# Hybrid encoder layer on one core: x transposed by TensorE, and the first eight projection steps in an order by hand

## The chip, the cores and the metric

The kernel runs on one core of one Trainium2 chip. A core has five engines with instruction streams of their own: TensorE (PE in the profile; its weight loads are shown apart as PEld), VectorE (DVE), ScalarE (ACT), GpSimd (POOL) and SyncE (SP). They meet through semaphores, and they share an on-chip memory (SBUF), the accumulators behind TensorE (PSUM) and the DMA queues to and from HBM. The metric is the device time of one execution, in microseconds (us), over several executions of the same program. Lower is better.

## The reference

One layer of an encoder over 1024 tokens of 1024 features, in float32:

```python
h = rmsnorm(x, norm_gain)
q_a, k_a, v_a, g_a, q_b, k_b, v_b, g_b = split(h @ w_in)     # 512,128,128,512,512,512,512,512
q_a = rmsnorm(q_a by head, q_norm_a); k_a likewise           # 8 query heads, 2 key heads, 64 wide
q_a = q_a * cos + rotate_half(q_a) * sin; k_a likewise       # the rotation
o_a = softmax(q_a k_a^T / 8) v_a * silu(g_a)                 # full attention, 1024 keys
o_b = neighbourhood_attention(q_b, k_b, v_b, rpb) * silu(g_b) # a window of 8 x 16 grid places
x = x + concat(o_a, o_b) @ w_out
return rmsnorm(x, final_norm_gain)
```

Every large product is kept close to float32 by splitting both factors into a float16 value (hi) and the float16 rest (lo), and adding three products: hi by hi, lo by hi, hi by lo.

## The kernel before, in words

**Tiles and groups.** The tokens stand in eight tiles of 128, called x0 to x7. The columns of the weights stand in groups of 256. Group 0 (KVA) makes keys and values of head group A, groups 1 and 2 (QA, QA+1) its queries, four heads each; 3 to 12 make head group B and the gates, 13 to 16 are `w_out`. A projection works on two tokens' tiles at once, called a pair `up` of 0 to 3. One tile takes 3 products x 8 slices of 128 features = 24 matmuls of 128x256, a pair 48, and a pair's 48 are cut into 8 chunks of 6. So "k2" below is group 0 on pair 2 (x4 and x5), and "q2" is group 1 on it. The first pairs come in the order k0, q0, k1, q1, k2, k3, q2, q3, then the four pairs of group 2. TensorE does 72 chunks (nine pairs) before the first score of head group A. In the listings `pj0_3` is the PSUM tile of group 0, pair 3 (k3), `pj1_2` that of q2, `pj2_0` that of the first pair of group 2. Two PSUM banks hold these tiles in turn.

**From x to the projection.** A tile of x is loaded by SP, squared and summed by ACT (L303), turned into a scale by DVE and POOL (L310 to L312), scaled by DVE (L315), rounded to hi by ACT (L316), and the rest is taken by DVE or POOL (L320). Both halves are turned by a DMA transpose on SP's queue (L324) into `hT`, with features on the partitions; there are 16 such DMAs. The weights of a group go through squares (`prep_a`, or L372 in quarters, ACT), a sum on TensorE (L388), a power on POOL (L391), hi on ACT (L397 or L414) and lo on DVE (L404 or L419), and some small DVE work (`prep_e`, L436 to L443).

**From the projection to the score.** When a pair of k or q is done, ACT takes it out of PSUM (L598 for v, L550 copy and L551 squares; part a), DVE sums the squares (L554, L555) and POOL raises them to the power -1/2 (L556; part b). The rotation is part c: a product on DVE (L560), two on POOL (L564, from the tables), one on DVE (L567) and a sum on POOL (L568). Then ACT rounds to hi (L583 for q; L608 and L609 for k), DVE takes the rest (L584; L614), and SP issues a DMA transpose (L587; L620 and L622). The tables of cos and sin are first multiplied by the gains: `tables()` on DVE (L279 to L289), `scale_tab` on POOL (L292, four times). A score of head group A multiplies a tile of queries by the keys of all 1024 tokens (L741, L743), in two halves, so the second matmul of the first score needs the keys of k3. DVE takes its maximum (L748), ACT the exponentials (L752) and their rounding (L753), DVE the rest (L758), SP issues the transpose, and TensorE multiplies by v (L775, L776).

**What sets the order.** `Flow` is the order by hand: slots, one to a pair, and in each slot positions ("pre", "mid", "post", "end"). `at(delay, position, work)` puts work into a later slot, `fill(n)` issues n chunks of matmuls, and `step(n)` runs a whole slot. TensorE's order is always the written one. For the other engines it is the written one inside blocks marked `manual_schedule`; outside, a scheduler orders them by its own estimates. The first pairs are outside. Weights of groups 2 and 3 (1 MB each) are loaded through POOL's queue, held back by a copy on POOL that needs x6 and x5 (`gate`, L220).

## Time and profile before

| what | us |
|---|---|
| three runs | 556.81, 555.02, 556.80 (median 556.8) |
| the profiled execution | 554.79 |
| its span, first to last instruction | 553.0 |
| first matmul of a projection | 14.64 |
| k3's values leave PSUM (ACT, L598) | 69.14 |
| SP issues the transpose of k3's keys (L620) | 76.97 |
| first score (L741) | 87.15 |

The span is the time between the first and the last instruction of the profiled execution; its own time is 1.8 us longer. In listings of groups, a row has the line of the source, the engine, the operation, the tile written and the tile read with their sizes and the count; behind the bar the busy time, the mean of one in ns, and the idle time just ahead of them with what ended it. In a timeline a row begins with its start and its length, rows that follow at once are joined (x8), and the brackets hold the idle time ahead and what ended it. In the table by stretches each engine has its busy time and its number of instructions, then come the granted clock of TensorE, the share of the DMA engines, and GB/s.

### The profile page before, as it was taken

Reading aid. Unit: us, or ns where it says so; the run is one execution under the profiler, and the core shown is the slowest. Engines: PE = TensorE matmul, PEld = TensorE weight load, DVE = VectorE, ACT = ScalarE, POOL = GpSimd, SP = SyncE. Lnnn points to the kernel's source line nnn. Section 1 sums busy time; section 2 is a strip of 40 time slices with the busy share of each in tenths; the row PEclk is TensorE's granted clock in tenths of the full one; section 3 lists DMA queues with packets and bytes.
Section 4 is the critical chain, followed back from the end, with each engine's and each line's share of the span. In section 5 each row is a group of like instructions: output and inputs, shape, how many; then the busy total and the mean of one; then the engine's idle time right before and its main releaser. Section 6 shows DMA issues by size and latency. Waiting matters only on the chain.

```text
span 553.0 us, 12864 instructions
## 1 busy us (share of the span) xinstructions
PE 507.8 (92%) x5071; PEld 397.2 (72%) x5071; DVE 445.3 (81%) x887; ACT 381.4 (69%) x671; POOL 178.9 (32%) x201
## 2 busy tenths in 40 slices
PE   2657889998999999999999999999999998799994
PEld 0446768876887555558888888988777786589883
DVE  4599678889987888879879898867898997887732
ACT  4545465967887868787787696648688788784411
POOL 1385787581110000101000022634433123344510
PEclk9989999999999999999999999999999999999998
DMA  8997837879999999999997999744897799979722
GB/s 243 210 203 216 146 59 181 135 144 176 208 196 217 191 231 186 216 176 178 194 217 143 202 186 200 120 125 71 146 191 138 136 250 202 219 115 204 173 74 76
DMA packets 244509, 95.40 MB, mean 173 GB/s; under 512 B 235489, under 2 KB 236001, under 8 KB 242530
## 3 DMA queue, kind: packets, MB, share of 16 engines
q1 hardware_dynamic: 242434, 81.23, 80.1%
q0 software_dynamic: 1728, 12.58, 7.3%
q8 instruction: 39, 0.64, 0.5%
q10 hardware_dynamic: 288, 0.79, 0.5%
q14 instruction: 20, 0.16, 0.1%
HBM read 29.56 MB, written 4.19 MB: 61 GB/s over the span
## 4 chain that ended last, share of the span: by engine, by line
PE 50%; DVE 10%; ACT 9%; issue 5%; DMA 3%; POOL 0%; DVEq 0%; POOLq 0%; ACTq 0%
PE pj L504 17%; PE kb L504 7%; PE pjb L504 7%; PE pv L775 5%; PE s L741 4%; PE s L743 4%; ACT rq L856 3%; DVE ar L854 3%; ACT ar L858 2%; PE pv L776 2%; PE sb L504 2%; DMA pt<-ar 2%; DVE ar L863 1%; DMA ar<-ar 1%; DVE whl L419 1%
## 5 line engine op out<-in xcount | busy, mean ns | idle before, releaser
L504 PEld LDWEIGHTS <-hT 128*128 128x128 f16 x2112 | 204.2, 99 | 59.5 <-DMA hT<-ar 16.3
L504 PE MATMUL pj<-whl,hT 128*128 128x256 f16 x1680 | 201.7, 278 | 21.8 <-DMA hT<-ar 9.4
L752 ACT ACTIVATE ar<-s,nm,sm 128x1024 f32<-128x1024 f32 x64 | 76.9, 1201 | 47.7 <-DVE nm L748 45.7
L748 DVE CUSTOM_DVE_ANT_0 ar<-s,sm 128x1024 bf16<-128x1024 f32 x64 | 82.0, 1281 | 30.3 <-PE s L743 28.5
L504 PEld LDWEIGHTS <-ar 128*128 128x128 f16 x768 | 73.8, 98 | 16.0 <-issue 7.8
L758 DVE TENSOR_TENSOR ar<-ar 128x1024 f16<-128x1024 f32 x64 | 79.4, 1241 | 1.2 <-ACT ar L753 1.2
L753 ACT ACTIVATE ar<-ar 128x1024 f16<-128x1024 f32 x64 | 67.6, 1057 | 2.3 <-DVE ar L758 0.4
L504 PE MATMUL pjb<-whl,ar 128*128 128x256 f16 x480 | 56.4, 273 | 2.8 <-ACT whl L414 1.5
L856 ACT ACTIVATE rq<-ar,nm 128x384 f32<-128x384 f32 (+1 forms) x64 | 34.0, 579 | 25.7 <-DVE nm L854 25.1
L504 PE MATMUL pjb<-whl,hT 128*128 128x256 f16 x432 | 50.4, 273 | 0.1
L784 POOL TENSOR_TENSOR ar<-ar,sum 128x256 f32<-128x256 f32 x16 | 11.3, 709 | 110.7 <-DVE ar L783 95.3
L504 PE MATMUL kb<-hT,whl 128*128 128x512 f16 x192 | 44.5, 379 | 0.0
L419 DVE SCALAR_TENSOR_TENSOR whl<-raw,sm,whl 128x512 f16<-128x512 f32 x52 | 41.0, 821 | 2.7 <-ACT whl L414 2.7
L775 PE MATMUL pv<-va,ar 128*128 128x128 f16 x384 | 39.1, 220 | 0.0
L863 DVE SCALAR_TENSOR_TENSOR ar<-rq,ar 128x768 f16<-128x768 f32 (+1 forms) x32 | 29.3, 915 | 11.0 <-ACT ar L858 10.6
L741 PE MATMUL s<-kTa,rq 128*128 128x512 f16 x128 | 38.1, 379 | 0.0
L776 PE MATMUL pv<-va,ar 128*128 128x64 f16 x384 | 37.8, 193 | 0.0
L775 PEld LDWEIGHTS <-ar 128*128 128x128 f16 x384 | 33.9, 98 | 5.3
L776 PEld LDWEIGHTS <-ar 128*128 128x128 f16 x384 | 33.2, 98 | 5.3
L414 ACT ACTIVATE whl<-raw,sm 128x512 f16<-128x512 f32 x52 | 34.0, 709 | 1.4 <-POOL sm L391 1.4
L391 POOL TENSOR_TENSOR sm<-wss,mh 128x1 f32<-128x1 f32 x17 | 10.5, 619 | 72.7 <-DVE wss L390 72.7
L910 POOL TENSOR_TENSOR ar<-ar,qkg 128x256 f32<-128x256 f32 x16 | 17.1, 1072 | 51.6 <-DVE qkg L908 36.4
(174 smaller groups left out, 915.9 us busy)
## 6 DMA issues: line engine op xcount, KB each, us to landing
raw<-in_w_dram POOLq DMA_DIRECT2D x11, 1024.0 KB, 7.6
ar<-in_x_dram SPq DMA_DIRECT2D x7, 512.0 KB, 6.1
raw<-in_wo_dram SPq DMA_DIRECT2D x3, 1024.0 KB, 7.0
khh<-ar SPq DMA_DIRECT2D x16, 128.0 KB, 2.7
x2b<-in_x_dram SPq DMA_DIRECT2D x4, 512.0 KB, 7.4
x<-in_x_dram SPq DMA_DIRECT2D x4, 512.0 KB, 5.6
out_dram<-x2b SPq DMA_DIRECT2D x8, 256.0 KB, 4.1
out_dram<-x SPq DMA_DIRECT2D x7, 256.0 KB, 2.9
```

The lines of the kernel that those rows point to most:

```text
L414: act.activation(wp[g][0][:, q], raw[g][:, q], AF.Copy, scale=col(S_ + g))
L419: dve.scalar_tensor_tensor(wp[g][1][:, q], raw[g][:, q], col(S_ + g), wp[g][0][:, q], op0=OP.mult, op1=OP.subtract)
L504: pe.matmul(*o[0], **o[1])
L741: pe.matmul(s[:, c * 512:(c + 1) * 512], q, kTa[:, 4 * c:4 * c + 4, hh], start=True, stop=False)
L748: dve.tensor_tensor_reduce(out=hl[:, 1].bitcast(BF16), in0=s, in1=col(SHA).to_broadcast([P, 1024]), scale=col(NSA), scalar=3e38, op0=OP.ad ...
L752: act.activation(p32, s, AF.Exp, bias=nm, scale=col(SCA), accum_out=rsum[hh, u][:, h:h + 1])
L753: at(0, "mid", lambda: act.activation(hl[:, 0], p32, AF.Copy))
L758: dve.tensor_tensor(hl[:, 1], p32, hl[:, 0], op=OP.subtract)
L775: pe.matmul(o, pt[:, kt], va[:, kt, hh], start=kt == 0, stop=False)
L776: pe.matmul(o[:, :D], pt[:, 8 + kt], va[:, kt, hh, :D], start=False, stop=kt == 7)
L856: act.activation(p32[:, e], t[:, e], AF.Exp, bias=nm, scale=-1.0)
L863: dve.scalar_tensor_tensor(hl[:, 1], p32, 2.0 ** 14, hl[:, 0], op0=OP.mult, op1=OP.subtract)
```

## The change

It has three parts.

1. **TensorE turns x.** For each tile, after the scaling, eight transposes of 128x128 in float32 (`tp`, a matmul against an identity that POOL builds at the start) go into one PSUM tile `xT`, ACT rounds PSUM to the hi half of `hT` in two instructions of 128x512 (`tp_hi`), and DVE subtracts to get the lo half, 128x1024 (`tp_lo`). The 16 DMA transposes, the rounding in SBUF and the subtraction in SBUF are gone. There is one `xT`, so the transposes of a tile follow the `tp_lo` of the tile ahead of it. Twenty matmuls of 128x256 on the identity, whose result nobody reads (`busy`), are issued ahead of the first transposes.
2. **The first eight steps in an order by hand.** Before the loop all engines' work up to the second projection pair is put into `manual_schedule`, and `stage(1)` to `stage(7)` write out where the work of each tile, of the tables and of groups 2 and 3 stands among the chunks. `tables()` and the four `scale_tab` stand behind `tp_lo(6)`, in stage 4. Groups 2 and 3 are loaded through SP's queue, without the copies on POOL; the squares of group 2 come in quarters, and its rounding (`prep_c`, `prep_d`) stands in stage 6, behind k3. The split of group 3 comes behind the first score, where it came ahead of it. Group 4's load is issued by POOL in stage 7.
3. **Rotations later.** `lag` moves part c, and what follows it, by more slots: for keys of pairs 0 to 3 by 4, 2, 1, 1 where it was 0, for queries of group 1 by 3, 2, 1, 1. Part b moves from "mid" to a new position "b" ahead of "post". Group 2 stays.

```diff
-        (sp if "b" in late else pool).dma_start(raw[g], w[g] if g < 13 else wo[g - 13])
+        (sp if "b" in late or g < 4 else pool).dma_start(raw[g], w[g] if g < 13 else wo[g - 13])
...
+    def tp(u, *ks):
+        if not xT:
+            xT.append(ps_s.tile([P, KC, P], F32, tag="s", name="xT"))
+        for k in ks:
+            pe.transpose(xT[0][:, k], xts[u][:, k * P:(k + 1) * P], ident)
+
+    def tp_hi(u, half):
+        ks = slice(4 * half, 4 * half + 4)
+        act.activation(hT[0][:, ks, u * P:(u + 1) * P], xT[0][:, ks], AF.Copy)
+
+    def tp_lo(u):
+        cs = slice(u * P, (u + 1) * P)
+        dve.tensor_tensor(hT[1][:, :, cs], xT[0], hT[0][:, :, cs], op=OP.subtract)
+
+    def busy(n):
+        b = ident.bitcast(BF16)
+        for _ in range(n):
+            pe.matmul(spare[0][:, :256], b[:, :P], b, start=True, stop=True)
...
+    def lag(g, up):
+        return 1 if g > QA else {KVA: (4, 2, 1, 1), QA: (3, 2, 1, 1)}[g][up]
...
-        at(1, "post" if g == QA + 1 else "mid", b)
-        at(2 if g == QA + 1 else 1, "post", c)
+        at(1, "post" if g == QA + 1 else "b", b)
+        at(1 + lag(g, up), "post", c)
...
-                at(2, "pre", hi)
+                at(2 + lag(KVA, up), "pre", hi)
...
+            if i == 4:
+                yield "pre mid b"
+                x_scale(7)
+                yield 2
+                tp(6, *range(8))
+                split_t(6)
+                tables()
+                for k in (2, 3, 0, 1):
+                    scale_tab(k)
+                yield "post"
+                yield 6
+            if i == 5:
+                tp(7, *range(8))
+                yield "pre mid"
+                split_t(7)
+                yield "post b"
+                yield 8
+            if i == 6:
+                yield "pre"
+                prep_c(2)
+                yield "mid"
+                prep_d(2)
+                yield "b post"
+                yield 8
+            if i == 7:
+                yield "pre"
+                load_w(4)
+                yield "mid b post"
+                yield 8
...
+        for i in range(1, 8):
+            fl.slot += 1
+            for todo in stage(i):
+                if isinstance(todo, int):
+                    fl.fill(todo)
+                else:
+                    for pos in todo.split():
+                        fl.run(pos)
+            fl.run("end")
+        fl.slot += 1
+
     fl.step(PAIR)
```

What this does to the order is seen at two places. The first is POOL around the tables and the rotations of the keys, in the kernel before. `tabs` are the tables, `nt0_2` is the sum of squares of k2, `nt0_3` of k3, `nt1_2` of q2, `sm` small scales; `ar` is the common area, in which the rotated tiles lie (128x4x32 and 128x256 are keys, 128x8x32 and 128x512 queries).

```order
L564 TENSOR_TENSOR ar_78<-ar_78,tabs_98 128x4x32 x2
L568 TENSOR_TENSOR ar_78<-ar_78 128x256
L391 TENSOR_TENSOR sm_97<-wss3_0_313,mh_83 128x1
L556 TENSOR_TENSOR nt0_3_647<-nt0_3_647,mh_83 128x4
L564 TENSOR_TENSOR ar_78<-ar_78,tabs_98 128x4x32 x2
L568 TENSOR_TENSOR ar_78<-ar_78 128x256
L556 TENSOR_TENSOR nt1_2_725<-nt1_2_725,mh_83 128x8
```

And POOL at the same place after the change, from the four table products to k3's sum (the line numbers are the changed kernel's: L296 was L292, L597 was L564, L601 was L568, L589 was L556; `raw4` is the load of group 4).

```order
L296 TENSOR_TENSOR tabs_100<-tabs_100,qkg_87 128x512 x4
L597 TENSOR_TENSOR ar_78<-ar_78,tabs_100 128x4x32 x2
L601 TENSOR_TENSOR ar_78<-ar_78 128x256
L597 TENSOR_TENSOR ar_78<-ar_78,tabs_100 128x8x32 x2
L601 TENSOR_TENSOR ar_78<-ar_78 128x512
L597 TENSOR_TENSOR ar_78<-ar_78,tabs_100 128x4x32 x2
L601 TENSOR_TENSOR ar_78<-ar_78 128x256
L589 TENSOR_TENSOR nt0_2_621<-nt0_2_621,mh_85 128x4
L589 TENSOR_TENSOR nt0_3_705<-nt0_3_705,mh_85 128x4
L597 TENSOR_TENSOR ar_78<-ar_78,tabs_100 128x8x32 x2
L601 TENSOR_TENSOR ar_78<-ar_78 128x512
L597 TENSOR_TENSOR ar_78<-ar_78,tabs_100 128x4x32 x2
L601 TENSOR_TENSOR ar_78<-ar_78 128x256
L221 DMA raw4_804<-in_w_dram 128x2048
L589 TENSOR_TENSOR nt1_2_798<-nt1_2_798,mh_85 128x8
L597 TENSOR_TENSOR ar_78<-ar_78,tabs_100 128x4x32 x2
L589 TENSOR_TENSOR nt1_3_873<-nt1_3_873,mh_85 128x8
L597 TENSOR_TENSOR ar_78<-ar_78,tabs_100 128x8x32 x2
L601 TENSOR_TENSOR ar_78<-ar_78 128x256
```

Before, k3's power was followed at once by k3's two products and its sum. Now the rotations of k0, q0 and k1 stand behind the tables in one row; the powers of k2 and k3 stand side by side behind them, and between k3's power and its sum stand the whole rotations of q1 and k2, the powers of q2 and q3, and two products of q2.

The second place is ACT around k3, in the kernel before: `va` takes the values, L550 and L551 are part a, L608 and L609 the hi of keys.

```order
L598 ACTIVATE va_104<-pj0_3_598 128x4x64
L550 ACTIVATE ar_78<-pj0_3_598 128x256
L551 ACTIVATE ar_78<-pj0_3_598 128x256
L583 ACTIVATE ar_78<-ar_78 128x8x64
L608 ACTIVATE ar_78<-ar_78 128x2x2x64
L609 ACTIVATE ar_78<-ar_78 128x2x2x64
L550 ACTIVATE ar_78<-pj1_2_670 128x512
```

And after the change: L641 and L642 are the hi of keys (first k1's, then k2's, last k3's), L616 the hi of queries, L631 to L584 part a, L431 the rounding of group 2's weights (`whl2`), L404 the squares of group 4 in quarters.

```order
L641 ACTIVATE ar_78<-ar_78 128x2x2x64
L642 ACTIVATE ar_78<-ar_78 128x2x2x64
L631 ACTIVATE va_106<-pj0_3_656 128x4x64
L583 ACTIVATE ar_78<-pj0_3_656 128x256
L584 ACTIVATE ar_78<-pj0_3_656 128x256
L431 ACTIVATE whl2_714<-raw2_220,sm_99 128x1024 x2
L583 ACTIVATE ar_78<-pj1_3_824 128x512
L584 ACTIVATE ar_78<-pj1_3_824 128x512
L616 ACTIVATE ar_78<-ar_78 128x8x64
L641 ACTIVATE ar_78<-ar_78 128x2x2x64
L642 ACTIVATE ar_78<-ar_78 128x2x2x64
L583 ACTIVATE ar_78<-pj1_2_749 128x512
L584 ACTIVATE ar_78<-pj1_2_749 128x512
L583 ACTIVATE ar_78<-pj2_0_895 128x512
L404 ACTIVATE va_106,wss4_0_806<-raw4_804 128x512
L404 ACTIVATE va_106,wss4_1_807<-raw4_804 128x512
L404 ACTIVATE va_106,wss4_2_808<-raw4_804 128x512
L404 ACTIVATE va_106,wss4_3_809<-raw4_804 128x512
L641 ACTIVATE ar_78<-ar_78 128x2x2x64
L642 ACTIVATE ar_78<-ar_78 128x2x2x64
```

Part a of k3 stands behind the hi of k1 now, and k3's own hi stands behind the rounding of group 2, part a of q2 and q3, and the squares of group 4, which need that group's load to have landed.

More of the change, by code (lines that the diff above doesn't have):

```diff
@@ L141, in step @@
         self.run("mid")
+        self.run("b")
         self.work("dve")
@@ L229 @@
     dve.memset(ones, 1.0)
+    ident = carve(ar, MIX + 2048, [P], F32)
+    pool.memset(ident, 1.0)
+    pool.affine_select(out=ident, in_=ident, pattern=[[-1, P]], compare_op=OP.is_equal, fill=0.0, base=0,
+                       channel_multiplier=1)
     mh = one.tile([P, NU], F32, name="mh")
@@ L317, in x_y, with x_scale, x_hi @@
         x_t(u, 0)
+    def x_scale(u):
+        dve.scalar_tensor_tensor(xts[u], xts[u], xr[u][:, 1:], gain, op0=OP.mult, op1=OP.mult)
+    def x_hi(u):
+        act.activation(xhl[u][:, 0], xts[u], AF.Copy)
+        x_t(u, 0)
+    def tp(u, *ks):
[13 more added lines that the diff above has]
+            pe.matmul(spare[0][:, :256], b[:, :P], b, start=True, stop=True)
+    xT = []
     def x_lo(u, e):
@@ L392, in prep_b, with prep_c @@
         scaled.add(g)
-    def prep_c(g):
-        for i in range(0, KC, KC // 2):
+    def prep_c(g, halves=(0, 1)):
+        if g not in wp:
+            alloc_wp(g)
+        for i in [KC // 2 * h for h in halves]:
             s = slice(i, i + KC // 2)
@@ L1069 @@
         load_w1(2, 3)
+        load_x(2)
+        load_x(3)
         x_rs(0)
-        x_y(0)
+        x_scale(0)
+        busy(20)
+        tp(0, 0, 1, 2)
         prep_a2(0)
         prep_b(0)
+        tp(0, *range(3, 8))
         x_sq(1, act)
-        prep_c(0)
+        load_x(4)
+        tp_hi(0, 0)
+        prep_c(0, (0,))
         x_rs(1)
-        load_x(2)
-        x_lo(0, dve)
-        x_y(1)
-        load_x(3)
-        prep_a(1)
-        x_lo(1, pool)
-        prep_d(0)
+        x_scale(1)
@@ L1084 @@
+        tp_hi(0, 1)
+        prep_c(0, (1,))
+        tp_lo(0)
+        prep_d(0)
+        k, q = [kva_gen(up) for up in UP], group(1, [qa_gen(0, up) for up in UP])
+        fl.add(k[0], q[0], k[1], q[1], k[2], k[3], q[2], q[3], *group(2, [qa_gen(1, up) for up in UP]))
+        fl.fill(1)
+        prep_a(1)
+        tp(1, *range(8))
+        fl.fill(3)
+        load_x(5)
+        tp_hi(1, 0)
+        tp_hi(1, 1)
+        tp_lo(1)
         tables_in()
+        load_w(2)
+        prep_b(1)
+        fl.fill(4)
@@ L1085 @@
         x_sq(2, act)
-        load_x(4)
         x_rs(2)
-        load_x(5)
-        prep_e(0)
+        prep_c(1)
+        x_scale(2)
+        prep_d(1)
         x_sq(3, act)
-        x_y(2)
         x_rs(3)
-    k, q = [kva_gen(up) for up in UP], group(1, [qa_gen(0, up) for up in UP])
-    fl.add(k[0], q[0], k[1], q[1], k[2], k[3], q[2], q[3], *group(2, [qa_gen(1, up) for up in UP]))
-    fl.step(PAIR)
-    prep_b(1)
-    prep_c(1)
-    x_y(3)
-    x_lo(3, dve)
-    x_sq(4, act)
-    tables()
@@ L1102, with split_t @@
-    scale_tab(2)
-    x_rs(4)
-    x_y(4)
-    x_lo(4, dve)
-    x_lo(2, dve)
-    x_sq(5, act)
-    x_rs(5)
-    load_x(6)
-    scale_tab(0)
-    x_y(5)
-    prep_d(1)
-    x_sq(6, act)
-    x_lo(5, dve)
-    x_rs(6)
-    x_y(6)
-    x_lo(6, dve)
-    load_x(7)
-    scale_tab(3)
-    x_sq(7, dve)
-    prep_e(1)
-    gate[2] = 6
-    scale_tab(1)
-    x_rs(7)
-    x_y(7)
-    load_w(2)
-    gate[3] = 5
-    x_lo(7, dve)
-    load_w(3)
-    for p in range(8):
-        fl.step(PAIR)
+        def split_t(u):
+            tp_hi(u, 0)
+            tp_hi(u, 1)
+            tp_lo(u)
```

61 lines of the change are left out of this document (52 added, 9 removed).

## The prediction

> **What bounds the kernel now.** I read the busy shares, then the stretches between the marks of the start, then the waits, and last the timeline around k3 and the first score. A row of stretches gives for PE, PEld, DVE, ACT and POOL the busy time and the count, then granted clock, DMA share, GB/s.
>
> ```profile
> PE 507.8 (92%) x5071; PEld 397.2 (72%) x5071; DVE 445.3 (81%) x887; ACT 381.4 (69%) x671; POOL 178.9 (32%) x201
> 14.60:69.10 54.50, 39.96 (x308) 32.32 (x309) 42.12 (x81) 28.34 (x50) 35.29 (x41) 0.97 0.93 195
> 69.10:87.15 18.05, 15.67 (x132) 13.18 (x130) 14.66 (x34) 10.15 (x21) 15.49 (x16) 0.91 0.39 90
> 87.15:134.70 47.55, 45.44 (x434) 36.49 (x431) 42.85 (x67) 37.62 (x67) 28.67 (x22) 1.00 0.87 154
> 134.70:553.00 418.30, 402.80 (x4196) 314.00 (x4196) 339.90 (x696) 297.96 (x527) 96.40 (x115) 0.99 0.90 173
> ```
>
> TensorE sets the time: from the first score (87.15) to the end it lacks 2.1 of 47.55 us and 15.5 of 418.3. What can be won is in the first 69.1 us, where it is idle for 14.5 of 54.5 us. From there to the score only 2.4 of 18.05 are idle, but POOL is busy for 15.49 of them. Who is late in the first stretch, the waits say (total, times, longest):
>
> ```profile
> PE pj L504 <- DMA hT<-ar: 9.4, 4, 3.1
> PE pj L504 <- ACT whl L397: 6.7, 2, 5.5
> ```
>
> The four waits for transposed x are 9.4 us; the two for hi weights are 6.7, and the long one, 5.5, is for group 1.
>
> **The change part by part.** I work with T, the end of k3's matmuls, 69.1 now, and with the way from T to the first score, 18.05 now.
>
> *How early T comes.* The rows:
>
> ```profile
> 10.66 1.06 ACT L316 ACTIVATE ar<-ar 128x1024 f16<-128x1024 f32 x1 [1.54 <-DVE ar L315]
> 12.26 0.55 POOL L391 TENSOR_TENSOR sm<-wss,mh 128x1 f32<-128x1 f32 x1 [3.01 <-DVE wss L390]
> 12.85 2.19 ACT L397 ACTIVATE whl<-raw,sm 128x1024 f16<-128x1024 f32 x2
> 14.64 1.89 PE L504 MATMUL pj<-whl,hT 128*128 128x256 f16 x8 [2.65 <-DMA hT<-ar]
> 59.82 9.99 PE L504 MATMUL pj<-whl,hT 128*128 128x256 f16 x90
> L775 PE MATMUL pv<-va,ar 128*128 128x128 f16 x384 | 39.1, 220 | 0.0
> 2.40 3.75 PE L242 MATMUL gain_p<-gain_i,ar 1*128 1x512 f32 x4 [2.40 <-DMA gain_i<-in_gain_in_dram]
> 42.20 1.35 DVE L305 CUSTOM_DVE_ANT_0 ar<-ar 128x1024 bf16<-128x1024 f32 x1 [0.61 <-DMA ar<-in_x_dram]
> ```
>
> Without the DMA, the first matmul waits for the weights: group 0's scale is there at 12.81 (12.26 + 0.55), its first half of hi takes 2.19 / 2, so it starts at about 14.1; x0's own transposes lie ahead of that, since x0 is scaled by 10.66. The 288 matmuls of k0 to k3, q0 and q1 take 288 x 9.99 / 90 = 32.0. New on TensorE are 56 float32 transposes (x1 to x7), which the trace has not. From below, 39.1 / 384 = 0.10 each, the 128x128 float16 matmul (L775). From above, the float32 product of L242: 3.75 us for 2 x 512 columns, so 0.47 for 128 columns. I take 0.20, nearer the lower end, for L242 runs at the cold start, where the eight matmuls at 14.64 take 1.89 / 8 = 0.236 against 0.111 later: half of 0.47 is 0.23. So 56 x 0.20 = 11.2 (5.6 to 26.3). I add 2.5 for some 20 matmuls at the cold rate (20 x 0.125) and 1.2 for group 0's lo on DVE: T = 14.1 + 32.0 + 11.2 + 2.5 + 1.2 = 61.0, so 8.1 earlier than now (55.4 to 76.1 by the ends). The wait for group 1's weights I take as gone, since their sum and rounding now stand ahead of the scaling of x2 and x3; if it stayed, T would be 5.5 later. The twenty `busy` matmuls cost nothing: they end before x0 is scaled. Loading cannot hold this up: x7's load is in by 42.20, and x7 is wanted at about T - 8 = 53. Groups 2 and 3 on SP's queue rather than POOL's are ready well ahead of their use too.
>
> [...]
>
> *What then takes the place of the transposes.* The rotations now wait for the tables, and these stand behind `tp_lo(6)`. Their prices:
>
> ```profile
> L550 ACT ACTIVATE ar<-pj 128x512 f32<-128x512 f32 x7 | 4.1, 585 | 4.5 <-PE pj L504 4.5
> L320 DVE TENSOR_TENSOR ar<-ar 128x1024 f16<-128x1024 f32 x7 | 9.0, 1283 | 0.0
> 25.86 0.35 DVE L279 TENSOR_REDUCE sm<-qkg 128x1 f32<-128x64 f32 x2 [0.71 <-DMA qkg<-in_qk_gain_dram]
> 29.35 0.73 DVE L289 TENSOR_SCALAR qkg<-qkg,sm 128x64 f32<-128x64 f32 x4
> 38.08 1.26 POOL L292 TENSOR_TENSOR tabs<-tabs,qkg 128x512 f32<-128x512 f32 x1
> 60.49 0.86 POOL L564 TENSOR_TENSOR ar<-ar,tabs 128x128 f32<-128x128 f32 x2
> 61.43 0.73 POOL L568 TENSOR_TENSOR ar<-ar 128x256 f32<-128x256 f32 x1
> 63.99 1.85 POOL L564 TENSOR_TENSOR ar<-ar,tabs 128x256 f32<-128x256 f32 x2 [1.83 <-DVE ar L560]
> 67.04 1.27 POOL L568 TENSOR_TENSOR ar<-ar 128x512 f32<-128x512 f32 x1
> 69.14 0.36 ACT L598 ACTIVATE va<-pj 128x256 f16<-128x256 f32 x1
> L404 DVE SCALAR_TENSOR_TENSOR whl<-raw,sm,whl 128x1024 f16<-128x1024 f32 x4 | 6.3, 1571 | 0.0
> 71.48 0.21 DVE L555 TENSOR_SCALAR nt<-nt,sm 128x4 f32<-128x4 f32 x1
> 71.77 1.45 POOL L556 TENSOR_TENSOR nt<-nt,mh 128x4 f32<-128x4 f32 x1 [0.52 <-DVE nt L555]
> 75.63 1.64 POOL L556 TENSOR_TENSOR nt<-nt,mh 128x8 f32<-128x8 f32 x1
> L554 DVE TENSOR_REDUCE nt<-ar 128x8 f32<-128x512 f32 x7 | 4.7, 678 | 2.9 <-ACT ar L551 2.9
> L608 ACT ACTIVATE ar<-ar 128x256 f16<-128x256 f32 x4 | 1.7, 419 | 2.3 <-POOL ar L568 2.3
> L614 DVE TENSOR_TENSOR ar<-ar 128x256 f16<-128x256 f32 x8 | 3.0, 416 | 1.2 <-ACT ar L609 1.2
> 76.97 1.21 SPq L620 DMA_TRANSPOSE kTa<-ar  x1
> kTa<-ar SPq DMA_TRANSPOSE x4, 2.7
> 87.15 0.59 PE L741 MATMUL s<-kTa,rq 128*128 128x512 f16 x2
> ```
>
> A rotation of a key pair costs POOL 0.86 + 0.73 = 1.6 behind its power (1.45), of a query pair 1.85 + 1.27 = 3.1 behind 1.64. I follow the chain by the order of the changed kernel:
>
> - Behind x6's transposes TensorE has six chunks, eight transposes and eight chunks up to T: 14 x 6 x 0.111 + 8 x 0.20 = 10.9, so x6 is turned at T - 10.9.
> - Its split: 2 x 0.585 + 1.28 (L550's and L320's price, same sizes) = 2.5; `tables()` 2.4, an estimate from the rows at 25.86 and 29.35 (1.1) and nine single-column steps of 0.15 (L555, with four or eight columns, takes 0.21 and more): T - 6.0. Four tables on POOL, 4 x 1.26 = 5.0: T - 1.0.
> - POOL turns k0, q0, k1: 1.6 + 3.1 + 1.6 = 6.3: T + 5.3.
> - ACT rounds k1 (2 x 0.42) and only then takes out k3 (3 x 0.36 = 1.1), so k3's values leave PSUM at T + 6 in place of T + 0.04; then group 2's hi, 2.2: T + 9.4.
> - DVE has the second half of group 2's lo (1.6), five single-column steps (0.8) and only then k3's sum (half of L554's 0.68, and L555's 0.21: 0.6): T + 12.4.
> - POOL: k3's power 1.45, q1 3.1, k2 1.6: T + 18.6.
> - ACT: k2's hi 0.84, q2's part a 1.2; DVE: two sums for q2 and q3, 1.4, and q2's scale 0.2: T + 22.2.
> - POOL: q2's power 1.64, k3's products 0.86, q3's power 1.64, q2's products 1.85, and at last k3's sum 0.73: T + 28.9.
> - k3's hi 0.84, its lo 0.83, the transpose's 2.7 to its landing: T + 33.3. Some sixteen changes of engine at 0.1 each (DVE ends at 71.69, POOL begins at 71.77): T + 35.
>
> So the first score comes at 61 + 35 = 96, not at 87.15. Group 4's load is a second way to the same place: POOL issues it behind k2 (T + 18.6), and its squares stand ahead of k3's hi on ACT.
>
> ```profile
> raw<-in_w_dram POOLq DMA_DIRECT2D x4, 1024.0 KB, 7.3
> 32.62 4.04 PE L504 MATMUL pj<-whl,hT 128*128 128x256 f16 x20 [5.49 <-ACT whl L397]
> ```
>
> It lands at about T + 26, and four squares of about 0.6 each (L550's size) end at T + 28.4: just level with the chain, so I add nothing, but where the load is late it decides.
>
> *What is lost by it.* TensorE has only q2, q3 and the first pair of group 2 between T and the score, 144 x 0.111 = 16.0, and waits for the second of them until k3 is taken out, for the third until group 2's lo. Today that fills the 18.05; in 35 us 19 are idle. After the score the written work is the same, and the stretch behind has only 2.1 us of idle time to give back: +8.9. Behind an idle time the rate is low at first (20 matmuls in 4.04 at 32.62 are 0.20 each): 20 x 0.09 = +1.8, about 1.5 of it counted. Group 3's split (four L404-like halves, about 3.3 on DVE) moves behind the score, where DVE is busy for 42.85 of 47.55, and about 3 us of rotation work moves ahead of it: nothing net. Sum +8.9 + 1.5 = +10.4. The profiled execution's own time is 554.8 (span 553.0), so it would be 565.2; that execution is 2.0 below the median of the runs, 556.8, and I forecast 566 for the median, between 565.2 and 567.2.
>
> **The rivals.**
>
> *Faster: the rotations keep up.* If POOL's rotations go by as the pairs come, the chain is as long as today (T + 18) and the first score is at 61 + 18 = 79, so -8: 548. The point from which this decides is a chain shorter than 87.15 - 61 = 26. For it: in the row of the second stretch POOL is not yet the bound (15.49 of 18.05), and the powers of k0 to q1 now fall ahead of the tables, in POOL's idle time. Against it: POOL's work alone from the tables to k3's sum is 5.0 + 6.3 + 2 x 1.45 + 4.7 + 2 x 1.64 + 1.85 + 1.6 = 25.6; from T - 6 it ends at T + 19.6, and with hi, lo and transpose (4.4) the score is at T + 24 if POOL never waits. That alone would be -2, and the chain has three waits for ACT and DVE in it.
>
> *The same.* Transposes at the lower bound and less waiting ahead of T (T about 54) with the chain as forecast: 54 + 35 = 89, +1 to +3, within 0.5%, which is 2.8 us and about what a measurement of this kernel can tell from no change.
>
> *Dear transposes.* At 0.47 each T is 76, the first score at 111, and the time near 581. The row at 2.40 speaks for it, the cold start in it against.
>
> *The clock falls during the steps.* If transposes count as idle time for the clock, matmuls behind them run at 0.2 for some us. Seven groups, each followed by some 20 at 0.20 rather than 0.111, cost 7 x 1.8 = 12.6: T is 74, 578. In rows, idle times of 2.65 to 5.49 were followed by matmuls of 0.20 to 0.236; transposes of 1.6 are shorter than these. [...]
>
> *The change doesn't do what it says* is no rival here: the 16 DMA transposes are gone from the order.
>
> **How the numbers follow.** The forecast has 0.54, faster 0.18, same 0.12, dear transposes 0.08, the falling clock 0.08. The forecast's own range is 558 to 575: T + 31 to T + 40 (L556 costs 1.99 on average where 1.64 was taken), T from 59 to 64. The whole range is 553 to 580: below it lies most of the faster rival, above it the two dear ones. Faster by over 0.5%: 0.18; within: 0.12; slower: 0.54 + 0.08 + 0.08 = 0.70.
>
> **What would show it.** Right: in the changed profile the waits for `hT` by DMA are gone, k3's values leave PSUM about 6 us after the last of k3's matmuls, the first score stands at 92 to 100, and ahead of it TensorE waits for k3's keys over 10 us; the transposes have a mean near 0.2 us. Wrong: a first score before 87 (the rotations keep up), transposes of 0.1 or 0.4, or a granted clock below 0.9 in the first stretch. If the score comes late and the time is not longer, the loss is given back behind it, and that term is the one that failed.

## The result and the profile after

The changed kernel takes 563.24 us (562.40 to 564.41), the kernel before beside it 555.91 (554.18 to 556.81): 1.0137 times as long, with an interval of 1.0102 to 1.0172. It is slower by 7.3 us; 566 was forecast, with its range 558 to 575. The profiled execution takes 563.26, its span is 561.5. Two executions further down, 575.28 with every transpose twice (the profiled one) and 558.90 with group 4's load behind the ninth step, fell into a slower state; the times given there leave them out.

The busy row of the page, then the stretches: the steps by hand, from there to the first matmul of the first score, to DVE's first maximum of a score (L781, L748 before), to its 17th, to the end. The second fence has the last two of the kernel before.

```profile
PE 520.7 (93%) x5158; PEld 408.8 (73%) x5158; DVE 447.3 (80%) x886; ACT 383.2 (68%) x687; POOL 168.1 (30%) x198
21.29:61.10 39.81, 39.76 (x367) 35.64 (x364) 32.30 (x71) 24.15 (x55) 20.61 (x28) 1.00 0.31 98
61.10:81.12 20.02, 13.59 (x97) 10.78 (x97) 13.55 (x28) 7.53 (x15) 11.54 (x14) 0.83 0.35 80
81.12:94.15 13.03, 1.88 (x8) 0.60 (x6) 8.57 (x10) 5.90 (x14) 12.40 (x12) 0.69 0.37 81
94.15:166.14 71.99, 67.68 (x669) 54.55 (x668) 64.20 (x111) 56.80 (x96) 25.64 (x24) 0.99 0.90 162
166.14:561.50 395.36, 381.78 (x3964) 296.98 (x3960) 318.20 (x654) 277.03 (x490) 95.20 (x111) 0.99 0.87 171
```
```profile
88.22:156.80 68.58, 66.35 (x661) 53.71 (x660) 62.87 (x107) 55.73 (x96) 29.69 (x24) 1.00 0.97 167
156.80:553.00 396.20, 380.82 (x3968) 296.19 (x3964) 318.84 (x655) 279.03 (x497) 94.58 (x112) 0.99 0.89 171
```

The steps by hand do what they are written for: from 21.29 to 61.10 TensorE is busy for 39.76 of 39.81 us, at the full clock. But from 81.12 to 94.15 it stands nearly still, while POOL is busy for 12.40 of 13.03. The first maximum of a score is 5.9 us later than before (94.15 against 88.22), from there to the 17th go another 3.4 (71.99 against 68.58), and 0.8 come back later (395.36 against 396.20): 8.5 in the span. TensorE's timeline ahead of the first score:

```profile
25.43 1.04 PE L334 MATMUL xT<-ar 128*128 128x128 f32 x8
...
49.64 1.04 PE L334 MATMUL xT<-ar 128*128 128x128 f32 x8
50.51 10.64 PE L534 MATMUL pj<-whl,hT 128*128 128x256 f16 x96
66.41 8.30 PE L534 MATMUL pj<-whl,hT 128*128 128x256 f16 x48 [5.26 <-DVE va L635]
75.89 5.40 PE L534 MATMUL pj<-whl,hT 128*128 128x256 f16 x48 [1.17 <-ACT ar L584]
81.12 0.38 PE L774 MATMUL s<-kTa,rq 128*128 128x512 f16 x1
92.66 0.61 PE L774 MATMUL s<-kTa,rq 128*128 128x512 f16 x1 [11.15 <-DMA kTa<-ar]
```

No wait for `hT` by DMA is left. The 96 matmuls at 50.51 are k3 and q2, so k3 ends at about 50.51 + 5.3 = 55.8 (T of the prediction); q3 waits for k3 to be taken out of PSUM, the first pair of group 2 for q3, and the second matmul of the first score for k3's keys, 11.2 us. Behind its wait q3 takes 8.30 where the pair behind it takes 5.40, in a stretch with a granted clock of 0.83; the chain below does not wait for it. The chain that ends there, from the timeline of the other engines:

```profile
51.11 5.31 POOL L296 TENSOR_TENSOR tabs<-tabs,qkg 128x512 f32<-128x512 f32 x4 [2.80 <-DVE qkg L293]
56.38 1.77 POOL L597 TENSOR_TENSOR ar<-ar,tabs 128x128 f32<-128x128 f32 x2
...
63.12 1.05 POOL L601 TENSOR_TENSOR ar<-ar 128x256 f32<-128x256 f32 x1
...
64.83 0.36 ACT L631 ACTIVATE va<-pj 128x256 f16<-128x256 f32 x1
...
66.81 2.48 DVE L438 SCALAR_TENSOR_TENSOR whl<-raw,sm,whl 128x1024 f16<-128x1024 f32 x2 [0.55 <-ACT whl L431]
...
70.86 1.38 POOL L589 TENSOR_TENSOR nt<-nt,mh 128x4 f32<-128x4 f32 x1 [5.71 <-DVE nt L588]
...
81.85 1.31 POOL L597 TENSOR_TENSOR ar<-ar,tabs 128x128 f32<-128x128 f32 x2
...
85.19 1.85 POOL L597 TENSOR_TENSOR ar<-ar,tabs 128x256 f32<-128x256 f32 x2
...
87.00 0.72 POOL L601 TENSOR_TENSOR ar<-ar 128x256 f32<-128x256 f32 x1
...
89.84 1.21 SPq L653 DMA_TRANSPOSE kTa<-ar  x1
```

These are the links of the prediction in its order: the tables (to 56.4), k0, q0 and k1 (to 64.2), k3's values out of PSUM (64.83), group 2's lo, k3's power (70.86), q1, k2 and q2's power, k3's two products (81.85), q3's power and q2's products (85.19), and only then k3's sum (87.00) and its transpose (89.84).

What is lost behind the score, the first matmuls there and TensorE's waits show:

```profile
93.91 3.95 PE L534 MATMUL pj<-whl,hT 128*128 128x256 f16 x24
124.11 0.59 PE L774 MATMUL s<-kTa,rq 128*128 128x512 f16 x2 [1.17 <-ACT ar L785]
135.73 0.81 PE L534 MATMUL pj<-whl,hT 128*128 128x256 f16 x6 [3.14 <-DVE ar L675]
```
```profile
126.06 0.81 PE L504 MATMUL pj<-whl,hT 128*128 128x256 f16 x6 [1.95 <-DVE wss L390]
134.82 0.82 PE L504 MATMUL pj<-whl,hT 128*128 128x256 f16 x6 [0.28 <-DVE ar L642]
```

The 24 matmuls behind the idle time take 3.95, at a granted clock of 0.66 (92.6 to 98), where the rate of 0.109 read at a clock of 1.00 (36 from 45.71 to 49.64) gives 2.6: 1.3 lost. The exponentials (L785) and the evacuation of group 3's first pair (L675, group 3's split is now done among the scores) cost 1.2 + 3.1 where the kernel before (second fence) waits 1.95 + 0.3: 2.0 more.

### The profile page after: what moved, and what is told of

It reads as the page before. It is cut to its first block, busy times and chain, and to the rows that moved or that the text cites. A ratio compares the mean times of both kernels' runs of the same rounds, so it can differ in the third digit from the quotient of the medians.

```text
span 561.5 us, 13028 instructions
## 1 busy us (share of the span) xinstructions
PE 520.7 (93%) x5158; PEld 408.8 (73%) x5158; DVE 447.3 (80%) x886; ACT 383.2 (68%) x687; POOL 168.1 (30%) x198
## 4 chain that ended last, share of the span: by engine, by line
PE 59%; DVE 14%; ACT 13%; issue 8%; POOL 5%; DMA 1%; POOLq 0%; DVEq 0%; ACTq 0%
PE pj L534 21%; PE pjb L534 9%; PE kb L534 7%; PE pv L808 5%; PE s L776 4%; PE s L774 4%; ACT rq L889 3%; PE pv L809 3%; ACT ar L891 2%; DVE ar L887 2%; PE sb L534 2%; POOL ar L597 2%; DVE whl L453 2%; DVE ar L781 1%; ACT whl L448 1%
## 5 line engine op out<-in xcount | busy, mean ns | idle before, releaser
L534 PEld LDWEIGHTS <-hT 128*128 128x128 f16 x2112 | 204.0, 99 | 42.8 <-issue 14.1
L785 ACT ACTIVATE ar<-s,nm,sm 128x1024 f32<-128x1024 f32 x64 | 76.9, 1201 | 52.6 <-DVE nm L781 49.7
L781 DVE CUSTOM_DVE_ANT_0 ar<-s,sm 128x1024 bf16<-128x1024 f32 x64 | 81.9, 1280 | 29.4 <-PE s L776 28.8
L774 PE MATMUL s<-kTa,rq 128*128 128x512 f16 x128 | 38.4, 381 | 12.3 <-DMA kTa<-ar 11.2
L817 POOL TENSOR_TENSOR ar<-ar,sum 128x256 f32<-128x256 f32 x16 | 10.9, 679 | 110.3 <-DVE ar L816 94.9
```

Source lines behind the costliest of these rows:

```text
L534: pe.matmul(*o[0], **o[1])
L774: pe.matmul(s[:, c * 512:(c + 1) * 512], q, kTa[:, 4 * c:4 * c + 4, hh], start=True, stop=False)
L781: dve.tensor_tensor_reduce(out=hl[:, 1].bitcast(BF16), in0=s, in1=col(SHA).to_broadcast([P, 1024]), scale=col(NSA), scalar=3e38, op0=OP.ad ...
L785: act.activation(p32, s, AF.Exp, bias=nm, scale=col(SCA), accum_out=rsum[hh, u][:, h:h + 1])
```

## The experiments

Theory 1 is the prediction's: the time is lost in the chain of rotations on POOL, ACT and DVE, which ends with k3's keys, because of the order in which the change writes it. The first rival is that TensorE's own new work, 64 transposes, is the loss; the second, that the later rotations are, whatever the order.

"The first score" at a time means its second matmul, the one that needs k3's keys. Positions are read from one profiled execution of each kernel, and T, the end of k3's matmuls, differs by up to 1.4 us between kernels that are alike up to there (why, the runs on the clock at the start show). So the way from T to the score shows an edit better than the score alone. Times are medians; the kernel before, measured again beside the runs, had medians of 555.2 to 556.0. The expectations call the runs by short names: e1 is the next one, e2 the sums ahead of group 2's rounding, e3 the tables in stage 2, e5 the four moves together, e6 the same with group 4's load moved as well, e10 the 16 matmuls at the start.

### k3's sum right behind its products

```diff
                 split_t(7)
+                fl.work("act")
                 yield "post b"
...
             fl.run("end")
         fl.slot += 1
+        fl.step(PAIR)
-    fl.step(PAIR)
```

> Edit: the ninth pair's step is written into the hand-ordered block too (and group 3's squares are issued by hand in stage 5), so that POOL does k3's sum right behind k3's two products, no longer behind q3's power and q2's products; two of group 4's four squares also move behind k3's hi on ACT. Theory 1 (the chain of rotations on POOL, ACT and DVE sets the first score): the changed kernel's trace has 3.8 us between the end of k3's products (83.2) and its sum (87.0), and these go, so k3's keys and the second matmul of the first score come at about 89 in place of 92.7, and the time falls by 3 to 4 us, to 559 to 560. Rival (the time is lost because TensorE does 64 transposes more, 0.11 us each, and all that waits behind them is slack): no change, 563. Rival (group 4's load and squares set the end of the chain): the gain stops at about 2 us, since the second square ends at about 84 and all four at 85.7.

Measured: 560.70 us, 1.0104 of the kernel before (1.0068 to 1.0141), so 2.5 below the changed kernel (by the medians, here and below). The second matmul of the first score comes at 87.56, 5.1 earlier:

```profile
49.14 10.64 PE L534 MATMUL pj<-whl,hT 128*128 128x256 f16 x96
87.56 0.61 PE L774 MATMUL s<-kTa,rq 128*128 128x512 f16 x1 [3.50 <-DMA kTa<-ar]
...
82.11 0.63 ACT L404 ACTIVATE va<-raw 128x512 bf16<-128x512 f32 x1 [5.19 <-DMA raw<-in_w_dram]
...
83.50 0.40 ACT L641 ACTIVATE ar<-ar 128x256 f16<-128x256 f32 x1
```

Of the 5.1, 1.4 are not the edit's: k3's matmuls begin at 49.14 instead of 50.51, though nothing ahead of them was edited. The way from T to the score is 3.7 shorter, as expected, and 2.5 of it reached the end. It speaks against the rival that names TensorE. The rival that names group 4 is true in part: k3's sum ends at 81.40 on POOL, but its hi (L641) stands on ACT behind two of group 4's squares, which wait for the load until 82.11, and begins at 83.50.

### k3's sum of squares ahead of group 2's rounding

```diff
             if i == 6:
-                yield "pre"
+                yield "pre mid b post"
                 prep_c(2)
-                yield "mid"
                 prep_d(2)
-                yield "b post"
```

> Edit: in stage 6 the sums of squares and the rotations due there (k3's sum, q1's and k2's rotation) are written ahead of group 2's rounding and lo, not behind them. Theory 1: in the changed kernel POOL idles for 5.7 us ahead of k3's power (65.15 to 70.86), since DVE first does group 2's lo and five small steps (66.8 to 70.1); k3's power comes at about 66.5 and all behind it 4 to 5 us earlier: the second matmul of the first score at about 88, the time lower by about 4 us, 559. Group 2's lo moves to about 72, still ahead of the pair that needs it (75.9). Rival (TensorE's own work): no change, 563.

Measured: 560.41, 1.0101 (1.0063 to 1.0138), 2.8 below the changed kernel. The first score is 2.5 earlier, less than the 4 to 5 expected:

```profile
76.56 6.71 PE L534 MATMUL pj<-whl,hT 128*128 128x256 f16 x48 [3.48 <-ACT ar L584]
90.12 0.61 PE L774 MATMUL s<-kTa,rq 128*128 128x512 f16 x1 [6.63 <-DMA kTa<-ar]
```

k3's power does come 3.9 earlier (66.94 against 70.86). But the rotations of q1 and k2 behind it now run beside group 2's lo on DVE: they take POOL 6.5 us (68.30 to 74.78) where they took 4.6 (72.22 to 76.85), and the lo takes 3.95 where it took 2.48. In this order ACT also takes q3 out of PSUM behind k2's hi and q2, so the pair of group 2 waits 3.48 for it where it waited 1.17.

### The tables in stage 2

```diff
                 x_scale(5)
+                tables()
+                for k in (2, 3, 0, 1):
+                    scale_tab(k)
                 yield "mid b post"
...
                 split_t(6)
-                tables()
-                for k in (2, 3, 0, 1):
-                    scale_tab(k)
                 yield "post"
```

> Edit: the tables and their four products on POOL stand in stage 2, behind the scaling of x5, not in stage 4 behind x6's split; the rotations stay where they are. Theory 1: the tables leave the chain (POOL is idle around 32 to 37 us), so k0's products on POOL begin when DVE has done x7's split and k0's product, about 54.2 in place of 56.4: the first score 2 to 3 us earlier, the time 2 us lower, 561. If the tables were the whole of the loss, the time would fall by 5 us (four products of 1.3) or more. Rival (TensorE's own work): no change, 563.

Measured: 568.51, 1.0231 (1.0198 to 1.0263): 5.3 above the changed kernel, where 2 below was expected. That was wrong, and the timeline of this run shows why:

```profile
37.81 4.98 POOL L296 TENSOR_TENSOR tabs<-tabs,qkg 128x512 f32<-128x512 f32 x4 [5.54 <-DVE qkg L293]
...
44.36 0.56 POOL L315 TENSOR_TENSOR xs<-xs,mh 128x1 f32<-128x1 f32 x1
...
47.69 1.97 PE L334 MATMUL xT<-ar 128*128 128x128 f32 x8 [2.27 <-DVE xs L314]
...
54.15 1.04 PE L334 MATMUL xT<-ar 128*128 128x128 f32 x8
```

POOL has idle time there, but the power of x6's scale (L315) stands in its queue behind the four tables and a power of queries. x6 is scaled at 45.2, its transposes come at 47.69 (44.84 in the changed kernel) and x7's at 54.15 (49.64). The expectation counted POOL's idle time and not who is queued behind.

### The tables at the end of stage 3

```diff
                 prep_b(2)
+                tables()
+                for k in (2, 3, 0, 1):
+                    scale_tab(k)
                 yield 4
...
                 split_t(6)
-                tables()
-                for k in (2, 3, 0, 1):
-                    scale_tab(k)
                 yield "post"
```

> Edit: only the tables and their four products move, to the end of stage 3: ahead of x6's split, but behind x7's scale on POOL. e3, which put them in stage 2, was 5 us slower than the changed kernel: there the four products (37.8 to 42.8) stood ahead of the scales of x6 and x7 on POOL, x6's transposes came 2.8 us and x7's 4.5 us later than in the changed kernel. Theory 1: without that queue the move gains what e3 was to gain: k0's products at about 54 in place of 56.4, k3's values out of PSUM 2 to 3 us earlier, the first score 2 to 3 us earlier, the time lower by 1 to 3 us, 560 to 562. Rival (the tables are better off behind the splits wherever they stand, since DVE's 2.4 us are on the way): 565 or more.

Measured: 561.12, 1.0109 (1.0065 to 1.0154), 2.1 below the changed kernel, the first score at 90.26, 2.4 earlier. So the tables were about 2 us of the chain, and what made the run before 5.3 slower was the queue.

### Every transpose twice

```diff
         for k in ks:
-            pe.transpose(xT[0][:, k], xts[u][:, k * P:(k + 1) * P], ident)
+            for _ in range(2 if u else 1):
+                pe.transpose(xT[0][:, k], xts[u][:, k * P:(k + 1) * P], ident)
```

> Edit: every transpose of x1 to x7 is issued twice, with the same result. It measures what the transposes cost where they stand. In the changed kernel's trace eight take 0.87 us on TensorE's own row of matmuls (25.43 to 26.30), 0.109 each. Theory 1: x6's split, from which the chain of rotations starts, comes 48 x 0.109 = 5.2 us later and so does the first score: the time rises by 5 to 6 us, to 568 to 569, so that the 56 transposes of the changed kernel cost as much themselves. Rival (they lie in time in which TensorE waits anyway): under 2 us.

Measured: 568.66, 1.0234 (1.0194 to 1.0273), 5.4 above the changed kernel for 56 transposes: 0.10 each. Sixteen take 1.91 where eight took 1.04:

```profile
42.88 1.91 PE L335 MATMUL xT<-ar 128*128 128x128 f32 x16
...
97.08 0.61 PE L775 MATMUL s<-kTa,rq 128*128 128x512 f16 x1 [12.74 <-DMA kTa<-ar]
```

So the 56 transposes do cost about what they take on TensorE, 5 to 6 us; that alone does not decide between theory and rival, since the chain of rotations starts behind them. The next two runs decide.

### k3's rotation ahead of q2's power

```diff
             if i == 7:
                 yield "pre"
+                yield "mid post b"
                 load_w(4)
-                yield "mid b post"
```

> Edit: in stage 7 k3's rotation is written ahead of q2's sum and power, and group 4's load behind both; by the new order POOL does k3's products and sum together. Theory 1: q2's power (1.8) with the sums ahead of it on DVE (1.3) and the 3.8 us between k3's products and its sum leave the chain: the second matmul of the first score at about 86, the time lower by 3 to 6 us, 557 to 560. Rival (TensorE's own work): 563.

Measured: 558.31, 1.0034 (1.0007 to 1.0060): two lines in another order bring 4.9 of the 7.3 us back, with all 64 transposes in place. The second matmul of the first score comes at 87.30, 5.4 earlier, 1.1 of it ahead of the edit:

```profile
49.38 10.64 PE L534 MATMUL pj<-whl,hT 128*128 128x256 f16 x96
87.30 0.61 PE L774 MATMUL s<-kTa,rq 128*128 128x512 f16 x1 [7.32 <-DMA kTa<-ar]
```

k3's sum ends at 80.07 and SP issues the transpose of its keys at 81.60. It lands only 5.7 us later, beside the load of group 4, which POOL issues at 81.78; in the changed kernel, without that load beside it, the same transpose took 2.8 (89.84 to 92.66).

### The four moves together

The edits of the runs on k3's sum, on stage 6, on the tables in stage 3 and on stage 7 above, in one kernel.

> Edit: four moves together, nothing else: the ninth step by hand (as e1), the sums and rotations of stage 6 ahead of group 2's rounding (as e2), in stage 7 k3's rotation ahead of q2's sum and power, and the tables in stage 3 behind x7's scale, where no scaling of x is queued behind them on POOL (in e3 those of x6 and x7 were). Theory 1 (the chain of rotations sets the first score, and most of that moves the end): from 92.7 the chain loses 5.1 (measured in e1), 2.5 (e2), 1.8 + 1.3 (q2's power on POOL and two sums on DVE) and 2.3 (the tables): 80, and TensorE's own three pairs end at about 80 too. Of e1's 5.1 only 2.6 reached the end, so between half and all of 13 us does: 551 to 557, below the changed kernel by 6 to 12, and about level with the kernel before or up to 4 us faster. Rival (the transposes on TensorE are the loss): 563. Rival (what is moved ahead is paid back behind the score, where ACT and DVE are nearly full): 560 as e1 and e2.

Measured: 553.53, 0.9966 of the kernel before (0.9940 to 0.9992), 9.7 below the changed kernel. The first score stands at 81.43, and TensorE waits 1.4 us for k3's keys where it waited 11.2:

```profile
49.19 10.64 PE L534 MATMUL pj<-whl,hT 128*128 128x256 f16 x96
...
81.43 0.39 PE L774 MATMUL s<-kTa,rq 128*128 128x512 f16 x1 [1.40 <-DMA kTa<-ar]
```

T is at 54.4, so the way from T to the score is 27.0 in place of 36.9: 9.9 shorter, about as much as the time. The expectation's 13 counted the 1.4 at e1's start as the edit's. The lag of the rotations is as the change has it and the transposes are on TensorE; only the order among them is another. The transposes still cost their 5 to 6 us; they are a part of T, which is 14.7 earlier than before the change all the same. That settles it for theory 1.

### Group 4's load behind the ninth step as well

```diff
-                load_w(4)
...
         fl.step(PAIR)
+        load_w(4)
```

> Edit: e5 with group 4's load issued behind the ninth step instead of in stage 7, so that the load and its four squares (3 us of ACT) fall behind the first scores. Theory 1: the squares stood among the last links of the chain; without them ACT has 3 us less ahead of the first exponentials: 0 to 3 us below e5. Rival (group 4's weights are wanted soon after the scores begin, and come late): 1 to 5 us above e5.

Measured: 550.75, 0.9908 (0.9872 to 0.9943), 2.8 below the four moves alone, though the two intervals touch. It has the lowest median of all and is below both kernels: k3's keys are there when TensorE's own pairs end, and the first score comes without a wait:

```profile
80.12 0.59 PE L774 MATMUL s<-kTa,rq 128*128 128x512 f16 x2
```

The squares were not the reason: with the four moves they already stand behind the first exponentials (83.62; the first square is at 84.82). There the load was issued at 76.35 beside k3's transpose (76.10), which landed 5.3 us later; with the load moved it takes no more than 2.9. That makes the way from T to the score 1.8 shorter. Where the rest of the 2.8 lies, if it is more than noise, is open.

### The rotations back where they were

```diff
-        return 1 if g > QA else {KVA: (4, 2, 1, 1), QA: (3, 2, 1, 1)}[g][up]
+        return 1 if g > QA else {KVA: (0, 0, 0, 0), QA: (0, 0, 0, 0)}[g][up]
...
                 prep_e(0)
+                tables()
+                for k in (2, 3, 0, 1):
+                    scale_tab(k)
                 yield "b post"
...
                 split_t(6)
-                tables()
-                for k in (2, 3, 0, 1):
-                    scale_tab(k)
                 yield "post"
...
             if i == 5:
-                yield "post b"
+                yield "b post"
```

> Edit: the rotations back at the slots that they had before the change (all lags 0), the tables in stage 1 since they must precede them. Theory 1 with its reason for the lag: DVE and POOL work in order, so the first rotation waits on DVE for the tables (2.4 us) and then for k0's power behind four table products on POOL (5.2 us), with x3's split and x4's scaling queued behind it; each further pair holds the splits up by 1 to 3 us. k3's matmuls (55.9 in the changed kernel) end 8 to 14 us later, the first score is at 88 to 98, the time 558 to 570: undoing the lag is no gain above 5 us. Rival (the later rotations alone are the loss): k3's matmuls still end near 56, the first score comes at 74, where TensorE's three pairs end, and the time falls to about 545.

Measured: 566.80, 1.0187 (1.0148 to 1.0226): 3.6 above the changed kernel, the first score at 95.36.

```profile
37.91 0.42 DVE L593 TENSOR_TENSOR ar<-ar,nt 128x256 f32<-128x256 f32 x1 [4.65 <-POOL nt L589]
...
40.36 0.42 ACT L641 ACTIVATE ar<-ar 128x256 f16<-128x256 f32 x1 [11.99 <-POOL ar L601]
41.94 1.09 ACT L338 ACTIVATE hT<-xT 128x512 f16<-128x512 f32 x2
42.60 0.61 PE L534 MATMUL pj<-whl,hT 128*128 128x256 f16 x2 [9.96 <-ACT hT L338]
```

k0's first product waits on DVE for its power behind the tables, ACT waits 11.99 for k0's sum with a tile's split (L338) queued behind, and TensorE waits 9.96 for that. k3's matmuls end at 78.6, 22.8 later than in the changed kernel, more than the 8 to 14 expected; from there TensorE's own pairs run to the score without a wait for keys (95.36, T + 16.8). The second rival falls: the lag is what keeps the splits of x going, and is no loss by itself.

### The clock at the start

```diff
         tp(0, *range(3, 8))
+        busy(16)
```

> Edit: 16 more matmuls that nobody reads, behind x0's transposes, where TensorE waits for group 0's weights (12.2 to 13.9 in the changed kernel). There the granted clock is 0.50 from 15.3 to 19.6, and matmuls take 0.22, though TensorE had done 20 matmuls and 8 transposes up to 12.2. Theory (transposes don't count as work for the clock, so it falls some 4 us behind the last real matmul, at 10.5): the clock stays at 1.0, x1's transposes take 1.0 in place of 1.9, the 18 matmuls behind them 2.1 in place of 3.9; all behind is 2 to 3 us earlier, the time 560 to 561. Rival (the clock falls by the time since the start, or by the waits at 12.2 and 14.5): the same clock, 563 to 564.

Stretches of the changed kernel, and under them of this run (the column behind POOL is the granted clock):

```profile
14.40:14.70 0.30, 0.07 (x1) 0.07 (x1) 0.30 (x2) 0.30 (x1) 0.00 (x0) 0.50 1.19 273
17.00:19.00 2.00, 2.00 (x12) 1.47 (x11) 1.02 (x2) 1.51 (x5) 0.00 (x0) 0.50 0.98 227
```
```profile
17.00:19.00 2.00, 1.93 (x19) 1.58 (x18) 1.76 (x2) 2.00 (x5) 0.00 (x0) 1.00 1.02 240
```

The clock stays at 1.00, and the first score comes at 90.88, 1.8 earlier. Why it stays is not shown: the 16 matmuls add work and fill an idle time of 1.7 as well. But the time is 563.22, 1.0147 (1.0108 to 1.0186): no gain in the median.

The changed kernel's profile flatters this comparison. In it and in the nine kernels above, which share its first matmuls, the clock fell to 0.50 at 13.5 to 16.0 and stayed there for 3.4 or 6.8 us; in the changed kernel it was 6.8 (14.4 to 21.2), in e1 3.4, and e1's T is 1.4 earlier. In the kernel without the lag the eighteen matmuls at 17.58 take 2.55 where those of the changed kernel, at 17.48, take 3.94, also 1.4 less. So the 16 matmuls gain 0.8 to 2.1 us of T (53.6 against 54.4 to 55.8), not always 2 to 3.

The same line added to the kernel with the four moves and group 4's later load:

> Edit: e6 and e10's 16 matmuls together. Theory: as in e10 the first steps are 2 to 3 us earlier; in e6 TensorE's own pairs end with the chain, so most of it reaches the first score: 548 to 550 against 550.9 of e6. Rival (the splits of x or what lies behind the score bound it): 551.

Measured: 551.70, 0.9949 (0.9918 to 0.9979), the clock at 1.00 at the start again, the first score at 78.96 in place of 80.12, and nothing of it at the end. Both times the steps came earlier, and both times the time did not fall with them. The intervals reach some 2 us to either side, so a gain of 1 us can't be told from none; whether it is given back, and where, is open.

Last, the changed kernel without its first twenty:

```diff
-        busy(20)
```

> Edit: the twenty matmuls ahead of x0's transposes are left out. Theory as in e10: they raise the clock for x0's transposes and the first four matmuls only (0.8 us in eight transposes, 0.4 in four matmuls), and the clock falls again behind them; without them all is 0 to 1 us later, 563 to 564. Rival (they warm TensorE for the first pair): 2 to 4 us later, 565 to 567.

Without the twenty matmuls the time is 564.21, 1.0174 (1.0136 to 1.0213), 1.0 above the changed kernel, and the intervals overlap: as expected. The way is another than expected: there is no fall at the start (the clock reads 1.00 from 10.3 to 25.5), and the full rate comes only behind the first pair's beginning:

```profile
14.41 1.01 PE L534 MATMUL pj<-whl,hT 128*128 128x256 f16 x4 [1.72 <-ACT whl L431]
...
18.02 2.21 PE L534 MATMUL pj<-whl,hT 128*128 128x256 f16 x18
```

The four matmuls at 14.41 take 1.01 where the changed kernel's four at 13.88 take 0.60; the eighteen at 18.02 take 2.21 where those of the changed kernel, at 17.48, take 3.94.

### All runs side by side

| kernel | T, us | second matmul of the first score, us | time, us | of before |
|---|---|---|---|---|
| before | 69.1 | 87.4 | 555.9 | 1 |
| four moves, group 4 later, 16 matmuls at the start | 53.8 | 78.96 | 551.70 | 0.9949 |
| four moves, group 4 later | 54.9 | 80.12 | 550.75 | 0.9908 |
| four moves | 54.4 | 81.43 | 553.53 | 0.9966 |
| k3's rotation ahead of q2's power | 54.6 | 87.30 | 558.31 | 1.0034 |
| k3's sum behind its products | 54.4 | 87.56 | 560.70 | 1.0104 |
| stage 6 | 55.8 | 90.12 | 560.41 | 1.0101 |
| tables in stage 3 | 55.6 | 90.26 | 561.12 | 1.0109 |
| 16 matmuls at the start | 53.6 | 90.88 | 563.22 | 1.0147 |
| without the first twenty | 54.8 | 92.01 | 564.21 | 1.0174 |
| the change | 55.8 | 92.66 | 563.24 | 1.0137 |
| tables in stage 2 | 60.3 | 94.85 | 568.51 | 1.0231 |
| no lag | 78.6 | 95.36 | 566.80 | 1.0187 |
| transposes twice | 61.3 | 97.08 | 568.66 | 1.0234 |

From 79 to 97 the score moves by 18.1 and the time by 17.0: among the orders by hand the time follows the first score nearly one for one, give or take 2 us. The single moves of 2 to 3 us (k3's sum, stage 6, tables in stage 3) have intervals that overlap with the changed kernel's; k3's rotation ahead of q2's power and the kernels with the four moves stand clear of it. The kernel before stands 2 to 5 us below its neighbours in the table, in keeping with the 3 us that the changed order loses behind the score.

## Why the prediction was right, and where it was not

**The mechanism and its place** were right: the transposes as DMAs were the wait, they go, and the rotations behind the tables take their place. k3's values leave PSUM late, TensorE idles for 17.6 us between T and the score (5.26 + 1.17 + 11.15; 19 forecast), and what is lost there isn't given back.

**How early T comes: the price of a transpose failed.** The prediction took 0.20 for each, between 0.10 and 0.47, reasoning that half of the cold float32 product is 0.23. It is 0.109 in the trace (eight from 25.43 to 26.30) and 0.10 by doubling, the lower end; the prediction itself had named transposes of 0.1 as a sign of being wrong. So 56 cost 6.1 in place of 11.2, and T is 55.8 in place of 61.0, the whole difference. The other terms held: the first matmul at 13.88 (14.1 forecast), no wait for group 1's weights.

**The chain** was T + 35 and is T + 36.9. It starts as forecast (x6 is turned at 45.71, T - 10.1, against T - 10.9). The size that was off most is POOL's: the rotations of k0, q0 and k1 take 7.8 (56.38 to 64.17) where 6.3 was summed. k0's two products alone take 1.77, with DVE at work beside them, where 0.86 was read in a row beside which DVE stood idle (60.49, before). So k3's values leave PSUM at T + 9.0 and not at T + 6. From there to the score the forecast was 29 (T + 6 to T + 35), and 27.8 was measured (64.83 to 92.66). The two errors, T 5.2 too late and the chain 1.9 too short, made the forecast of the score 96 where 92.66 was measured.

**Behind the score** the prediction gave 1.5 for the cold clock and nothing net for group 3's split. The cold start measured 1.3, the waits for the split and the exponentials 2.0, of which 0.8 came back later: "nothing net" was wrong. So of the sum +10.4, the +8.9 ahead of the score measured 5.3 (92.66 against 87.4, the second matmul both times), and the 1.5 behind it about 3; the span grew by 8.5, the median of the times by 7.3. That 566 came within 3 us of the measured time is in part luck: T was 5.2 too late, and 1.9 in the chain and some 1.7 behind the score made up for most of it.

**The rivals.** Rotations that keep up: not seen; POOL is busy for 12.40 of the 13.03 us ahead of the first maximum. But it is what the other orders make of the change: with T at 55.8 the score comes earlier than before with a chain under 87.4 - 55.8 = 31.6, and the four moves have 27.0 (81.43, with T at 54.4). Cheap transposes with the chain as forecast was the rival of no change: its price of the transposes was right, but the waits ahead of T that it left out (cold matmuls: 3.94 for the eighteen at 17.48) stayed. Dear transposes and a falling clock through the steps: the row 21.29 to 61.10, with 48 of the transposes in it, has a granted clock of 1.00; it read 0.50 ahead of that row, from 14.4 to 21.2. Group 4's load, the "second way to the same place", lands at about 82.8 and its squares end at 85.8, 1.9 ahead of k3's hi (87.75), which waits for k3's sum: just not deciding, as forecast. In other orders it did decide: in e1 its squares held k3's hi back by 2.1, and with the four moves the load beside k3's transpose made it land 2.5 later.

## What to carry to other kernels

When a wait is taken out of the head of a kernel, follow the next instruction that TensorE will want (here k3's keys) backwards through every in-order queue; what the queue's neighbours do counts more than how early the producer is done. Idle time of an engine is no free place for moved work: look at who stands behind it in its queue, as the tables ahead of x6's scale showed. Deferring work by whole slots was right for the splits of x, but the deferred items must come out in the order in which they are wanted: keys that all scores need ahead of queries that one needs.
